# Weight sums for a seven-product matrix multiply: subtracting on VectorE, or adding while they are loaded

## The chip, the cores and the metric

One core of a Trainium2 chip runs one decoder layer as one program. The metric is the device time of one execution in microseconds (us), as the median of repeated runs. Engines: PE (TensorE matmuls), DVE (VectorE), ACT (ScalarE), POOL (GpSimd), SP (SyncE); the last two only issue transfers in the part of the kernel that matters here.

## The reference, cut to what matters

The layer normalises its input, makes one wide projection, runs two token mixers side by side (gated DeltaNet, block attention), and joins them. The change touches the joining part, for 256 tokens, a model width of 2048 and mixer outputs `oa`, `ob` of width 1024:

```python
u_a = oa @ w_branch_a                   # (256,1024) @ (1024,2048)
u_b = ob @ w_branch_b
merged = sigmoid(gate_a) * u_a + sigmoid(gate_b) * u_b
y = merged @ w_out                      # (256,2048) @ (2048,2048)
out = x + rms_norm(y, post_norm_w)
```

All of it is float32. Every float32 operand of a matmul is split into a high part that the matmul takes exactly and a low rest, and three products (high·high, high·low, low·high) are summed.

## The kernel before

**Weights.** Each weight block of 512 rows by 512 columns (1024 KB) is loaded by SP into one of three `raw` buffers (`load`, line 794, or `proj_n`, line 347), cast by ACT to a high part (`split`, line 226), and the low part is formed by DVE (line 227). The matmuls (line 148) take both. SP can load the next block into a `raw` buffer only when the last reader of the old block is done. The order of PE is pinned to that of the program; small jobs of the other engines are put between the matmuls by queues of generators that advance by a tick after each group of matmuls.

**Seven products instead of eight.** `oa @ w_branch_a` is done for two pairs of 512 columns (stages `ua0` and `ua2`), and the upper half of `merged @ w_out` for one pair (stage `y`). In each stage a 256 by 1024 operand times a 1024 by 1024 weight is cut into quarters A11 to A22 and B11 to B22, and the four result quarters c11 to c22 (one PSUM bank each) come out of seven products of quarters (Winograd's form of Strassen's scheme), where eight would be the plain way. Three of the seven take sums or differences of the weights' quarters, and the last one, p4, takes a combination of all four. `seven` (line 799) writes out this order: p1 (`raw`), other work, p5 (`tq[0]`), p6 (`tq[1]`), other work, p2 (`raw`, B21), p7 (`tq[2]`), other work, p3 (`raw`, B22), other work, p4 (`tq[1]` again). The other work is four blocks of a gate projection in the `ua` stages (gate0 to gate3; 24 matmuls each) and a block of another output quarter in the `y` stage.

**Where the combinations come from.** Each stage has three 1024 KB tiles `tq[0..2]`. POOL loads B12, B22 and B11 into them, three plain transfers (`fetch`, line 753). DVE then forms the differences in place, six instructions on half tiles, some groups of matmuls later (`differences`, line 758, waits in `T_WAIT`, line 32). The fourth combination overwrites `tq[1]` between p6 and p4: two DVE instructions subtract it from the `raw` block of B21 (`difference`, line 815, executed at line 817), so this `raw` buffer is held until then. One slice of `tq[0]` also keeps a copy (`s5`) of a PSUM bank that DVE adds into others (lines 808 and 823).

**Places.** The tiles of `ua0` lie in the buffers `g1` (`tq_g`, holding `tq[0]` and `tq[2]`) and `z2` (`tq_z`, holding `tq[1]`), fetched in `solve` (line 1004). Those of `ua2` and `y` lie in `z0`, `z1`, `z2` (`tq`), fetched by `next_differences` (line 879) as soon as the last readers of these buffers are done: for `ua2` these are the attention's last products (`z1`), its last transposes (`z0`) and p4 of `ua0` (`z2`). POOL works its transfers off in order; one that waits holds up those behind it. After the last stage's tiles POOL also loads `hx` (the residual's input) and `postw`.

Of the kernel before, what the change touches and what calls it, by code (L numbers as in the profile page):

```python
# [8 lines left out]
F32 = mybir.dt.float32  # L9
# [3 lines left out]
ALU = mybir.AluOpType  # L13
AX = mybir.AxisListType

P = 128
# [12 lines left out]
LC_WAIT = 3.5  # L29
INV = (0.6, 2)  # L30
SLOW = 8
T_WAIT = (5, 7, 7)
V_WAIT = 8
SV_WAIT = 1
OS_WAIT = 3
# [40 lines left out]
def hybrid_layer(  # L76
# [15 lines left out]
    nc = tc.nc  # L92
# [13 lines left out]
    wo = w_out.rearrange("o d f -> (o d) f")  # L106
# [639 lines left out]
    oaT = [None]  # L746

    oas, tqs = [], []
    formed = []
    sq = Queue()  # L750
    extra.append(sq)

    def fetch(tq, w, c, i):

        rs, cs = (0, 512, 0)[i], (c + (1, 1, 0)[i]) * 512
        nc.gpsimd.dma_start(tq[i], w[rs : rs + 512, cs : cs + 512].rearrange("(k p) c -> p k c", p=P))

    def differences(tq, c, wait):
        yield wait
        for o, a, b in ((0, 0, 2), (1, 1, 0), (2, 1, 2)):  # L760
            for u in range(2):
                us = slice(2 * u, 2 * u + 2)
                pin(nc.vector.tensor_tensor(tq[o][:, us], tq[a][:, us], tq[b][:, us], op=ALU.subtract))
                yield 1
        formed.append(c)

# [27 lines left out]
        nc.sync.dma_start(raw, w[h * 512 : (h + 1) * 512, c * 512 : (c + 1) * 512].rearrange("(k p) c -> p k c", p=P))  # L796
        return raw

    def seven(quarter, s_, tq, w, c, banks, name, fill=lambda i: None, done=lambda b: None):
        c11, c12, c21, c22 = banks  # L800
        s5 = tq[0][:, 0]
        product([quarter(0, 0)], load(w, 0, c, name), [c21], [True], f"{name}p1")
        fill(0)
        product([s_[0]], tq[0], [c12], [True], f"{name}p5")
        nc.scalar.copy(c11, c21)
        product([s_[1]], tq[1], [c21], [False], f"{name}p6")

        dq.add(steps(lambda: nc.scalar.copy(s5, c12), lambda: nc.vector.tensor_tensor(c12, c21, s5, op=ALU.add)))
        fill(1)
        dq.drain()  # L810
        raw21 = load(w, 1, c, name)
        product([quarter(0, 1)], raw21, [c11], [False], f"{name}p2")
        product([s_[2]], tq[2], [c21], [False], f"{name}p7")

        def difference(u):
            us = slice(2 * u, 2 * u + 2)
            pin(nc.vector.tensor_tensor(tq[1][:, us], raw21[:, us], tq[1][:, us], op=ALU.subtract))

        dq.add(
            steps(  # L820
                lambda: difference(0),
                lambda: difference(1),
                lambda: nc.vector.tensor_tensor(c22, c21, s5, op=ALU.add),
                lambda: done(c11),
            )
        )
        fill(2)
        product([s_[3]], load(w, 1, c + 1, name), [c12], [False], f"{name}p3")
        dq.drain()
        dq.add(steps(lambda: done(c12), lambda: done(c22)))  # L830
        fill(3)
        product([quarter(1, 1)], tq[1], [c21], [False], f"{name}p4")
        dq.add(later(lambda: done(c21)))
# [5 lines left out]
    def steps(*fs):  # L839
        for f in fs:  # L840
            yield 0.5
            f()
# [4 lines left out]

    def branch_pair(i):
        c = 2 * i
        while not oas or c not in formed:  # L850
            sq.tick()
            gq.tick()
        if not fourth:
            for q in aq + bq:
                q.drain()
            early.close()
            fourth.append(ctx.enter_context(tc.tile_pool(name="wx", bufs=1)))
        c11, c12, c21, c22 = (acc_tile(f"a_ua{c}_{n}") for n in ("11", "12", "21", "22"))
        place = {id(c11): (c, 0), id(c12): (c + 1, 0), id(c21): (c, 1), id(c22): (c + 1, 1)}

        def done(b):
            cc, t = place[id(b)]
            nc.vector.tensor_tensor(ga(cc, t), ga(cc, t), b, op=ALU.mult)


        quarter = quarters(hT)
        n, g, col = (("ga", 3, CGA), ("gb", 2, CGB))[i]
        pts = [aux_tile(f"a_{n}{g}_{t}") for t in range(NT)]

        def gate(h):  # L870
            raw = load(w_in[:, col : col + D], h, g, n)
            product([quarter(0, h), quarter(1, h)], raw, pts, [h == 0] * 2, f"{n}{g}_{h}")
            if h == 3:
                for t in range(NT):
                    nc.scalar.activation(gate_place(n, g, t), pts[t], AF.Sigmoid, scale=rstd[:, t : t + 1])

        seven(quarters(oaT[0]), oas, tqs[-1], wa, c, (c11, c12, c21, c22), f"ua{c}", fill=gate, done=done)

    def next_differences(w, c):


        for q in aq + bq:
            q.drain()
        tqs.append([big.tile([P, 4, 512], F32, tag=f"z{i}", name=f"tq{len(tqs)}_{i}") for i in range(3)])
        for i in (2, 0, 1) if len(tqs) == 2 else (1, 0, 2):
            fetch(tqs[-1], w, c, i)
        formed.clear()
        sq.add(differences(tqs[-1], c, T_WAIT[len(tqs) - 1]))

    def solve():  # L890
        oT = big.tile([P, H, 2 * S], F32R, tag="u1", name="oaT")
# [63 lines left out]
        def turned_outputs(ozs):  # L955


            a = {}
            for t in (1, 0):
                for g in range(2):  # L960
                    pt = aux_tile(f"ot_{t}_{g}")
                    for hh in range(4):
                        tr(pt[:, hh * P : (hh + 1) * P], ozs[t][:, g, hh, :], ident)
                    a[t, g] = pt.rearrange("p (h n) -> p h n", n=P)
                for g in range(2):
                    ks = slice(4 * g, 4 * g + 4)
                    halved(oT[:, ks, t * P : (t + 1) * P], oT[:, ks, S + t * P : S + (t + 1) * P], a[t, g])
                yield 1
            oa_f = big.tile([P, 2, 4, P], F32, tag="tv", name="oa_f")
            x, y = (oa_f[:, i] for i in range(2))  # L970
            nc.scalar.copy(x, a[1, 1])
            nc.vector.tensor_tensor(a[1, 1], a[1, 0], x, op=ALU.add)
            nc.scalar.copy(y, a[0, 0])
            nc.vector.tensor_tensor(a[0, 0], a[1, 1], y, op=ALU.subtract)
            nc.scalar.copy(x, a[0, 0])
            yield 1
            nc.vector.tensor_tensor(a[0, 1], a[0, 1], x, op=ALU.subtract)
            nc.vector.tensor_tensor(a[1, 0], y, a[1, 0], op=ALU.subtract)
            yield 1
            sums = [None] * 4  # L980
            for i, o, tag in ((0, (1, 1), "tt"), (1, (0, 0), "tw"), (3, (0, 1), None), (2, (1, 0), "tv")):
                if tag:
                    tl = big.tile([P, 2, 4, P], F32R, tag=tag, name=f"oas_{i}")
                    sums[i] = tl[:, 0], tl[:, 1]
                else:
                    sums[i] = [wk.tile([P, 4, P], F32R, tag="s", name=f"oas_{i}_{n}") for n in ("hi", "lo")]
                halved(*sums[i], a[o])
                yield 1
            oas.extend(sums)
# [10 lines left out]
        obs.append(big.tile([P, H, 2 * S], F32R, tag="g0", name="obT"))  # L1000
        tg = big.tile([P, 2, 4, 512], F32, tag="g1", name="tq_g")
        tz = big.tile([P, 4, 512], F32, tag="z2", name="tq_z")
        tqs.append((tg[:, 0], tz, tg[:, 1]))
        for i in (0, 2, 1):
            fetch(tqs[0], wa, 0, i)
        sq.add(differences(tqs[0], 0, T_WAIT[0]))
        yield OS_WAIT
        while attended[0] < H:
            yield 0.5
# [95 lines left out]
    for blk in ORDER:  # L1105
        n, c = blk[:2].rstrip("0123456789"), int(blk[-1])
        if n in ("q", "kq"):
            if n == "kq":
                keys(c)
            queries(c)  # L1110
        elif n in ("zg", "zm"):
            silu_gate(n, c)
        elif n == "v":
            values(c)
        elif n == "mv":
            attention_values(c)
        elif n == "mk":
            attention(c)
        elif n == "ua":
            branch_pair(c)  # L1120
        else:
            sigmoid_gate(n, {"ga": CGA, "gb": CGB}[n], c)
        if n == "ua":
            next_differences(*((wa, 2), (wo, 0))[c])


    gq.drain()
# [10 lines left out]
    def merge(c):  # L1138
# [14 lines left out]
                nc.scalar.copy(sf[:, t], p3)  # L1153
            yield 0.5
        if c == 1:
            nc.vector.tensor_tensor(sf[:, 2], p3s[1], sf[:, 1], op=ALU.add)
            nc.vector.tensor_tensor(sf[:, 3], sf[:, 2], sf[:, 0], op=ALU.subtract)
            yield 0.5
            nc.vector.tensor_tensor(sf[:, 1], sf[:, 0], sf[:, 1], op=ALU.subtract)
            nc.vector.tensor_tensor(sf[:, 0], p3s[0], sf[:, 3], op=ALU.subtract)  # L1160
            for i, j in enumerate((2, 3, 1, 0)):
                yield 1
                nc.scalar.copy(SH[i], sf[:, j])
# [20 lines left out]
        if i < 3:  # L1184
            third(1 + i)

    while not formed or not summed:
        mq.tick()
        sq.tick()
    c11, c12, c21, c22 = (acc_tile(f"a_y{n}") for n in ("11", "12", "21", "22"))  # L1190
    seven(quarter, list(zip(SH, SL)), tqs[-1], wo, 0, (c11, c12, c21, c22), "y", fill=beside)

    postw = big.tile([P, D], F32, tag="z2", name="postw")
    nc.gpsimd.dma_start(postw, post_norm_w.broadcast_to([P, D]))
# [104 lines left out]
```

## Time and profile before

| what | value |
|---|---|
| time, median of 3 runs | 771.48 us (771.03 to 771.73) |
| the profiled execution's own time | 772.1 us |
| span inside it that the profile covers | 770.4 us |
| mean granted TensorE clock | 0.996 |
| PE busy | 761.0 us (99%) |
| DVE busy | 565.7 us (73%) |
| ACT busy | 435.3 us (57%) |
| read from HBM | 148.04 MB |

The profiled execution is 0.6 us slower than the median. In the page's rows, `a<-b,c` is an instruction that writes tile `a` and reads `b` and `c`; times are counted from the span's start. "DMA share" is the mean busy share of the core's 16 DMA engines in a stretch; it can come out a little over 1. Ends of matmuls are modelled, so the distance between starts tells more than their length.

### The profile page before, as it was taken

To read this page: it belongs to the slowest core of one execution; us is meant where nothing else is said; L and a number is where in the kernel's file an instruction comes from. 1 tells how busy PE (TensorE), PEld (TensorE's weight loads), DVE (VectorE), ACT (ScalarE), POOL (GpSimd) and SP (SyncE) were. 2 spreads that over 40 slices of the span, in tenths; PEclk is the share of its full clock that TensorE was granted. 3 is DMA by queue.
4 is the path that set the end of the run, shared out by engine and by line. 5 is a ranking of instruction groups with operands and counts; after the bars stand their busy time and mean duration, and the time that the engine had idled before them with its cause. 6 is when DMAs were issued, how large, how long until landed. Compare 5 with 4: busy or idle time off the path is not lost.

```text
span 770.4 us, 10406 instructions
## 1 busy us (share of the span) xinstructions
PE 761.0 (99%) x3941; PEld 650.0 (84%) x3941; DVE 565.7 (73%) x918; ACT 435.3 (57%) x660; POOL 35.0 (5%) x63
## 2 busy tenths in 40 slices
PE   9999999999999999999999999999999999999995
PEld 8998988899888888888898888788888888888884
DVE  6878669885978898775557876686658676888753
ACT  6776665657655664554456574554455544555731
POOL 4000001112000000002001000000000000000000
PEclk9999999999999999999999999999999999999998
DMA  8585675467655556668437356667544955385912
GB/s 291 188 262 193 198 205 172 136 178 211 200 183 196 186 180 203 185 197 204 127 110 270 129 202 220 217 218 251 187 163 179 367 186 197 116 300 184 334 49 110
DMA packets 94808, 151.87 MB, mean 197 GB/s; under 512 B 3365, under 2 KB 49062, under 8 KB 94246
## 3 DMA queue, kind: packets, MB, share of 16 engines
q1 hardware_dynamic: 90022, 134.41, 54.0%
q0 software_dynamic: 4128, 15.74, 6.1%
q10 hardware_dynamic: 608, 1.06, 0.4%
q8 instruction: 31, 0.51, 0.3%
q14 instruction: 19, 0.16, 0.1%
HBM read 148.04 MB, written 3.15 MB: 196 GB/s over the span
## 4 chain that ended last, share of the span: by engine, by line
PE 94%; ACT 2%; DVE 2%; DMA 1%; issue 0%; POOL 0%; DVEq 0%; POOLq 0%
PE a_gb L148 11%; PE a_ga L148 11%; PE a_y L148 11%; PE a_mq L148 6%; PE a_mk L148 6%; PE a_k L148 6%; PE a_ub L148 6%; PE a_zm L148 6%; PE a_zg L148 5%; PE a_mv L148 5%; PE a_ua L148 5%; PE a_q L148 4%; PE a_v L148 4%; PE s L148 1%; PE ms L148 1%; PE po L148 1%
## 5 line engine op out<-in xcount | busy, mean ns | idle before, releaser
L148 PE MATMUL a_ga<-hi_ga,hT 128*128 128x512 f32 x256 | 82.1, 394 | 0.0
L148 PE MATMUL a_gb<-hi_gb,hT 128*128 128x512 f32 x256 | 80.2, 390 | 0.0
L227 DVE TENSOR_TENSOR lo_gb<-raw_gb,hi_gb 128x1024 fp32r<-128x1024 f32 x32 | 38.9, 1224 | 25.0 <-ACT hi_gb L226 24.9
L148 PEld LDWEIGHTS a_gb<-hi_gb,hT 128*128 128x128 f32 x256 | 48.0, 188 | 10.6
L148 PEld LDWEIGHTS a_ga<-hi_ga,hT 128*128 128x128 f32 x256 | 48.1, 188 | 10.1
L226 ACT CAST hi_gb<-raw_gb 128x1024 fp32r<-128x1024 f32 x32 | 33.3, 1051 | 35.6 <-PE a_gb L148 26.5
L226 ACT CAST hi_ga<-raw_ga 128x1024 fp32r<-128x1024 f32 x32 | 33.7, 1055 | 32.6 <-PE a_ga L148 13.7
L227 DVE TENSOR_TENSOR lo_ga<-raw_ga,hi_ga 128x1024 fp32r<-128x1024 f32 x32 | 38.9, 1222 | 17.9 <-ACT hi_ga L226 17.5
L148 PE MATMUL a_ga<-lo_ga,hT 128*128 128x512 f32 x128 | 50.1, 392 | 0.1
L148 PE MATMUL a_gb<-lo_gb,hT 128*128 128x512 f32 x128 | 50.1, 391 | 0.0
L148 PE MATMUL a_zg<-hi_zg,hT 128*128 128x348 f32 (+1 forms) x192 | 47.1, 322 | 0.0
L148 PE MATMUL a_mq<-hT,hi_mq 128*128 128x512 f32 x128 | 47.0, 408 | 0.0
L148 PE MATMUL a_mk<-hT,hi_mk 128*128 128x512 f32 x128 | 46.2, 402 | 0.0
L148 PE MATMUL a_y<-hi_y,mT 128*128 128x512 f32 x144 | 46.1, 392 | 0.0
L148 PE MATMUL a_q<-hT,hi_q 128*128 128x512 f32 x128 | 45.9, 398 | 0.0
L148 PE MATMUL a_v<-hT,hi_v 128*128 128x512 f32 x128 | 45.3, 398 | 0.0
L148 PE MATMUL a_ub<-hi_ub,obT 128*128 128x512 f32 x128 | 41.3, 395 | 0.0
L148 PE MATMUL a_k<-hT,hi_k 128*128 128x512 f32 x128 | 40.7, 400 | 0.0
L148 PE MATMUL a_zm<-hi_zm,hT 128*128 128x512 f32 x128 | 40.5, 392 | 0.0
L148 PE MATMUL a_mv<-hi_mv,hT 128*128 128x512 f32 x128 | 40.1, 391 | 0.0
L148 PE MATMUL a_v<-hT,lo_v 128*128 128x256 f32 x128 | 36.1, 282 | 0.1
L148 PE MATMUL a_q<-hT,lo_q 128*128 128x256 f32 x128 | 35.9, 280 | 0.0
(384 smaller groups left out, 1975.6 us busy)
## 6 DMA issues: line engine op xcount, KB each, us to landing
raw_ga<-in_w_in_dram SPq DMA_DIRECT2D x16, 1024.0 KB, 5.1
raw_gb<-in_w_in_dram SPq DMA_DIRECT2D x16, 1024.0 KB, 6.0
raw_y<-in_w_out_dram SPq DMA_DIRECT2D x15, 1024.0 KB, 5.3
raw_q<-in_w_in_dram SPq DMA_DIRECT2D x8, 1024.0 KB, 5.6
raw_mv<-in_w_in_dram SPq DMA_DIRECT2D x8, 1024.0 KB, 5.1
raw_v<-in_w_in_dram SPq DMA_DIRECT2D x8, 1024.0 KB, 5.6
raw_zm<-in_w_in_dram SPq DMA_DIRECT2D x8, 1024.0 KB, 5.0
raw_mq<-in_w_in_dram SPq DMA_DIRECT2D x8, 1024.0 KB, 5.8
```

The lines of the kernel that those rows point to most:

```text
L148: return pin(nc.tensor.matmul(*args, **kwargs))
L226: nc.scalar.copy(hi, raw)
L227: nc.vector.tensor_tensor(lo, raw, hi.bitcast(F32), op=ALU.subtract)
```

## The change

The signs of the scheme are turned: all combinations of the weights' quarters become sums (B11+B12 in `tq[0]`, B11+B12+B22 in `tq[1]`, B12+B22 in `tq[2]`, and for p4 `tq[1]` plus B21), and the subtractions move to the activations' combinations and the result banks, where additions and subtractions are exchanged one for one. The sums are then formed by POOL's transfers: the first quarter is loaded plainly, and each further one by a transfer that adds to its tile (`accum_op`). Per stage that is 3 plain and 4 adding transfers in `fetch`, and one more adding transfer (B21 onto `tq[1]`) issued after p6. The 24 DVE instructions of lines 763 and 817 go, and with them the queue `sq`, `formed` and `T_WAIT`.

```diff
-    def fetch(tq, w, c, i):
-        rs, cs = (0, 512, 0)[i], (c + (1, 1, 0)[i]) * 512
-        nc.gpsimd.dma_start(tq[i], w[rs : rs + 512, cs : cs + 512].rearrange("(k p) c -> p k c", p=P))
-    def differences(tq, c, wait):
-        yield wait
-        for o, a, b in ((0, 0, 2), (1, 1, 0), (2, 1, 2)):
-            for u in range(2):
-                us = slice(2 * u, 2 * u + 2)
-                pin(nc.vector.tensor_tensor(tq[o][:, us], tq[a][:, us], tq[b][:, us], op=ALU.subtract))
-                yield 1
-        formed.append(c)
+    def fetch(tq, w, c, order=(0, 2, 1)):
+        b11, b12, b21, b22 = (
+            w[r * 512 : (r + 1) * 512, (c + x) * 512 : (c + x + 1) * 512].rearrange("(k p) c -> p k c", p=P)
+            for r in range(2)
+            for x in range(2)
+        )
+        parts = [b11, b12], [b11, b12, b22], [b12, b22]
+        for n in range(3):
+            for i in order:
+                if n < len(parts[i]):
+                    nc.gpsimd.dma_start(tq[i], parts[i][n], **({"accum_op": ALU.add} if n else {}))
+        return b21
...
-    def seven(quarter, s_, tq, w, c, banks, name, fill=lambda i: None, done=lambda b: None):
+    def seven(quarter, s_, tq, b21, w, c, banks, name, fill=lambda i: None, done=lambda b: None):
...
-        dq.add(steps(lambda: nc.scalar.copy(s5, c12), lambda: nc.vector.tensor_tensor(c12, c21, s5, op=ALU.add)))
+        dq.add(steps(lambda: nc.scalar.copy(s5, c12), lambda: nc.vector.tensor_tensor(c12, s5, c21, op=ALU.subtract)))
+        nc.gpsimd.dma_start(tq[1], b21, accum_op=ALU.add)
         fill(1)
         dq.drain()
-        raw21 = load(w, 1, c, name)
-        product([quarter(0, 1)], raw21, [c11], [False], f"{name}p2")
+        product([quarter(0, 1)], load(w, 1, c, name), [c11], [False], f"{name}p2")
         product([s_[2]], tq[2], [c21], [False], f"{name}p7")
-        def difference(u):
-            us = slice(2 * u, 2 * u + 2)
-            pin(nc.vector.tensor_tensor(tq[1][:, us], raw21[:, us], tq[1][:, us], op=ALU.subtract))
-        dq.add(
-            steps(
-                lambda: difference(0),
-                lambda: difference(1),
-                lambda: nc.vector.tensor_tensor(c22, c21, s5, op=ALU.add),
-                lambda: done(c11),
-            )
-        )
+        dq.add(steps(lambda: nc.vector.tensor_tensor(c22, s5, c21, op=ALU.subtract), lambda: done(c11)))
...
-    def next_differences(w, c):
+    def next_sums(w, c):
...
-        for i in (2, 0, 1) if len(tqs) == 2 else (1, 0, 2):
-            fetch(tqs[-1], w, c, i)
-        formed.clear()
-        sq.add(differences(tqs[-1], c, T_WAIT[len(tqs) - 1]))
+        tqs.append((tq, fetch(tq, w, c)))
```

More of the change, by code (lines that the diff above doesn't have):

```diff
@@ L31 @@
 SLOW = 8
-T_WAIT = (5, 7, 7)
 V_WAIT = 8
@@ L748, in hybrid_layer @@
     oas, tqs = [], []
-    formed = []
-    sq = Queue()
-    extra.append(sq)
-    def fetch(tq, w, c, i):
-        rs, cs = (0, 512, 0)[i], (c + (1, 1, 0)[i]) * 512
-        nc.gpsimd.dma_start(tq[i], w[rs : rs + 512, cs : cs + 512].rearrange("(k p) c -> p k c", p=P))
-    def differences(tq, c, wait):
-        yield wait
-        for o, a, b in ((0, 0, 2), (1, 1, 0), (2, 1, 2)):
-            for u in range(2):
-                us = slice(2 * u, 2 * u + 2)
-                pin(nc.vector.tensor_tensor(tq[o][:, us], tq[a][:, us], tq[b][:, us], op=ALU.subtract))
-                yield 1
-        formed.append(c)
+    def fetch(tq, w, c, order=(0, 2, 1)):
[10 more added lines that the diff above has]
+        return b21
     def product(a, raw, banks, first, name):
@@ L849, in branch_pair @@
         c = 2 * i
-        while not oas or c not in formed:
-            sq.tick()
+        while not oas:
             gq.tick()
@@ L875, in gate @@
                     nc.scalar.activation(gate_place(n, g, t), pts[t], AF.Sigmoid, scale=rstd[:, t : t + 1])
-        seven(quarters(oaT[0]), oas, tqs[-1], wa, c, (c11, c12, c21, c22), f"ua{c}", fill=gate, done=done)
-    def next_differences(w, c):
+        seven(quarters(oaT[0]), oas, *tqs[-1], wa, c, (c11, c12, c21, c22), f"ua{c}", fill=gate, done=done)
+    def next_sums(w, c):
         for q in aq + bq:
             q.drain()
-        tqs.append([big.tile([P, 4, 512], F32, tag=f"z{i}", name=f"tq{len(tqs)}_{i}") for i in range(3)])
-        for i in (2, 0, 1) if len(tqs) == 2 else (1, 0, 2):
-            fetch(tqs[-1], w, c, i)
-        formed.clear()
-        sq.add(differences(tqs[-1], c, T_WAIT[len(tqs) - 1]))
+        tq = [big.tile([P, 4, 512], F32, tag=f"z{i}", name=f"tq{len(tqs)}_{i}") for i in range(3)]
+        tqs.append((tq, fetch(tq, w, c)))
     def solve():
@@ L971, in turned_outputs @@
             nc.scalar.copy(x, a[1, 1])
-            nc.vector.tensor_tensor(a[1, 1], a[1, 0], x, op=ALU.add)
+            nc.vector.tensor_tensor(a[1, 1], a[1, 0], x, op=ALU.subtract)
             nc.scalar.copy(y, a[0, 0])
@@ L976, in turned_outputs @@
             yield 1
-            nc.vector.tensor_tensor(a[0, 1], a[0, 1], x, op=ALU.subtract)
+            nc.vector.tensor_tensor(a[0, 1], a[0, 1], x, op=ALU.add)
             nc.vector.tensor_tensor(a[1, 0], y, a[1, 0], op=ALU.subtract)
@@ L1002, in solve @@
         tz = big.tile([P, 4, 512], F32, tag="z2", name="tq_z")
[L1003 to L1006, printed above, removed]
+        tq = tg[:, 0], tz, tg[:, 1]
+        tqs.append((tq, fetch(tq, wa, 0)))
         yield OS_WAIT
@@ L1123, in hybrid_layer @@
         if n == "ua":
-            next_differences(*((wa, 2), (wo, 0))[c])
+            next_sums(*((wa, 2), (wo, 0))[c])
     gq.drain()
@@ L1155, in merge @@
         if c == 1:
-            nc.vector.tensor_tensor(sf[:, 2], p3s[1], sf[:, 1], op=ALU.add)
+            nc.vector.tensor_tensor(sf[:, 2], sf[:, 1], p3s[1], op=ALU.subtract)
             nc.vector.tensor_tensor(sf[:, 3], sf[:, 2], sf[:, 0], op=ALU.subtract)
@@ L1159, in merge @@
             nc.vector.tensor_tensor(sf[:, 1], sf[:, 0], sf[:, 1], op=ALU.subtract)
-            nc.vector.tensor_tensor(sf[:, 0], p3s[0], sf[:, 3], op=ALU.subtract)
+            nc.vector.tensor_tensor(sf[:, 0], p3s[0], sf[:, 3], op=ALU.add)
             for i, j in enumerate((2, 3, 1, 0)):
@@ L1185, in beside @@
             third(1 + i)
-    while not formed or not summed:
+    while not summed:
         mq.tick()
-        sq.tick()
     c11, c12, c21, c22 = (acc_tile(f"a_y{n}") for n in ("11", "12", "21", "22"))
-    seven(quarter, list(zip(SH, SL)), tqs[-1], wo, 0, (c11, c12, c21, c22), "y", fill=beside)
+    seven(quarter, list(zip(SH, SL)), *tqs[-1], wo, 0, (c11, c12, c21, c22), "y", fill=beside)
     postw = big.tile([P, D], F32, tag="z2", name="postw")
```

## The prediction

> **What bounds the kernel now.** First the page's busy times and its chain, then the list of PE's waits, then a table of the three stages.
>
> ```profile
> span 770.4 us, 10406 instructions
> ...
> PE 761.0 (99%) x3941; PEld 650.0 (84%) x3941; DVE 565.7 (73%) x918; ACT 435.3 (57%) x660; POOL 35.0 (5%) x63
> ...
> PE 94%; ACT 2%; DVE 2%; DMA 1%; issue 0%; POOL 0%; DVEq 0%; POOLq 0%
> ```
> ```profile
> PE warm L148 <- DVE epst L182: 1.1, 1, 1.1
> ```
> ```profile
> 482.00:530.00 48.00, 47.91 (x209) 38.67 (x208) 35.05 (x34) 27.58 (x29) 0.75 (x1) 1.00 0.67 237
> 568.00:610.00 42.00, 42.00 (x185) 34.30 (x184) 32.02 (x31) 25.08 (x27) 2.25 (x3) 1.00 0.62 226
> 683.00:720.00 37.00, 37.00 (x167) 30.37 (x166) 30.34 (x30) 23.41 (x26) 1.26 (x2) 1.00 0.65 229
> ```
>
> The chain is PE for 94% of the span, and PE's only listed wait is 1.1 us at the start. The table's columns are PE, weight loads, DVE, ACT, POOL, clock, DMA share and GB/s: in the stages that the change touches (`ua0`, `ua2`, `y`) PE is busy all the time, DVE at most 82% (30.34 of 37), and the DMA engines about two thirds. So work taken from DVE is worth only what PE loses to it, and a delay of what PE reads counts in full.
>
> **The change part by part.**
>
> *DVE's 24 instructions go.*
>
> ```profile
> L763 DVE TENSOR_TENSOR tq<-tq,tq x12: 1218/1218/1220, 533.3 to 632.7; 128x1024 f32<-128x1024 f32 x12
> ```
> ```profile
> L817 DVE TENSOR_TENSOR tq_z<-raw_ua,tq_z x2: 1217/1218/1218, 504.2 to 505.4; 128x1024 f32<-128x1024 f32 x2
> ```
> ```profile
> 514.22 0.39 PE L148 MATMUL a_ga<-hi_ga,hT 128*128 128x512 f32 x1
> 514.44 0.47 PE L148 MATMUL a_ga<-lo_ga,hT 128*128 128x512 f32 x1
> 514.76 0.62 PE L148 MATMUL a_ga<-hi_ga,hT 128*128 128x512 f32 x2
> ```
>
> 18 at line 763 and 6 at line 817, 1.218 us each, are 29.2 us of DVE. All lie beside a full PE. What PE lost shows in the distances between its starts: 0.22 us is usual, 0.32 us at 514.44, where gate3's block came late because its `raw` buffer was B21's, held for line 817. The same slip can be lost once per stage: 3 x 0.1, and I take 0.2 us as the gain. The exchanged additions and subtractions cost the same instruction. In the order lists of both builds PE, ACT and SP have the same instructions in the same order; DVE lacks the 24, with two multiplications by the gate moved by one place; only POOL's list grows.
>
> *POOL's transfers* go from 9 of 1024 KB to 24: 9 plain, 15 adding. An adding one waits until the transfer before it on the same tile has landed; POOL works in order, so its wait holds the next ones. No run so far has an adding transfer. The nearest rows:
>
> ```profile
> tq<-in_w_branch_a_dram POOLq DMA_DIRECT2D x3, 1024.0 KB, 5.6
> ...
> hx<-in_x_dram POOLq DMA_DIRECT2D x1, 2048.0 KB, 8.4
> ```
> ```profile
> DMA to landing us min/median/max: 5.4/7.7/9.8
> ```
> ```profile
> 412.00:414.00 2.00, 2.00 (x15) 1.82 (x14) 2.00 (x8) 1.97 (x3) 0.00 (x0) 1.00 1.03 411
> 486.00:488.00 2.00, 2.00 (x10) 1.63 (x9) 0.27 (x2) 1.10 (x2) 0.00 (x0) 1.00 1.02 413
> 488.00:490.00 2.00, 2.00 (x11) 1.59 (x10) 1.20 (x1) 0.73 (x2) 0.00 (x0) 1.00 1.02 379
> 492.00:496.00 4.00, 4.00 (x19) 3.26 (x18) 3.22 (x4) 3.42 (x5) 0.00 (x0) 1.00 0.02 4
> 500.00:506.00 6.00, 6.00 (x28) 4.92 (x27) 4.37 (x5) 4.22 (x4) 0.00 (x0) 1.00 0.00 0
> 508.00:512.00 4.00, 4.00 (x19) 3.24 (x18) 3.80 (x5) 0.00 (x0) 0.00 (x0) 1.00 0.97 355
> ```
>
> At DMA share 1 the engines move about 400 GB/s, so a plain block takes 2.6 us of them. Call W the engine time of an adding block. Lower bound: the add is free, W = 2.6. Upper bound: the slowest landing of a line 756 transfer, 9.8. An add must fetch the weights and the tile, 2048 KB; `hx` is the only row of that size, and 1024 KB more take 8.4 - 5.4 = 3.0 us. I take W = 6.0, at the wide side of twice a block.
>
> The Trainium skill, "Collectives: The Full Stack", section "The bandwidth ceiling: the fold count and why AG ≠ RS ≠ AR", says that a DMA add is slow because of its two reads and not because of the sum (measured ratio 1.93); times 2.6 that is an estimate of 5.0, by which the sum below would end with a stall of 0 to 0.7 us.
>
> *The point where it decides: B21's add in `ua0`.* It must land between p6's last read and p4's first cast.
>
> ```profile
> 476.67 0.75 POOL L756 DMA_DIRECT2D tq<-in_w_branch_a_dram  x1 [61.71 <-PE po L148]
> 481.24 0.75 POOL L756 DMA_DIRECT2D tq<-in_w_branch_a_dram  x1 [3.82 <-PE pt L151]
> 518.66 0.75 POOL L756 DMA_DIRECT2D tq<-in_w_branch_a_dram  x1 [36.67 <-DVE lo_ua0p L227]
> 588.54 0.75 POOL L756 DMA_DIRECT2D tq<-in_w_out_dram  x1 [69.13 <-DVE lo_ua2p L227]
> ```
> ```profile
> 490.78 1.23 DVE L227 TENSOR_TENSOR lo_ua0p<-tq_z,hi_ua0p 128x1024 fp32r<-128x1024 f32 x1 [1.57 <-ACT hi_ua0p L226]
> ```
> ```profile
> L226 ACT CAST hi_ua0p<-tq_z x4: 1040/1048/1050, 486.9 to 514.9; 128x1024 fp32r<-128x1024 f32 x4
> ```
> ```profile
> 519.85 0.39 PE L148 MATMUL a_ua<-hi_ua0p,oaT 128*128 128x512 f32 x1
> 520.07 0.40 PE L148 MATMUL a_ua<-lo_ua0p,oaT 128*128 128x512 f32 x1
> ```
> ```profile
> 495.26 0.37 SPq L796 DMA_DIRECT2D raw_ua<-in_w_branch_a_dram  x1
> 506.66 0.37 SPq L796 DMA_DIRECT2D raw_ga<-in_w_in_dram  x1
> 507.76 0.37 SPq L352 DMA_DIRECT2D raw_gb<-in_w_in_dram  x1
> ```
>
> p6 has read its tile at 492.0. But in POOL's list of the changed build this add stands behind five transfers for `ua2`: B11 into `tq[1]` (476.67), B11 into `tq[0]` (481.24), then the first add to `tq[1]`, the add to `tq[0]`, the second add to `tq[1]`. This last one waits for the landing of the first. PE needs p4's low part at 520.07; less a cast (1.05), a subtraction (1.23) and two handovers of 0.04, the add may land at 517.7.
>
> At 488.0 the two plain fetches are through (413 GB/s before it). Gate2's load (2.6, the 379 GB/s row) and the first add (6.0) end at 496.6; the second add and B21's follow into the queue. Then come three adds (18.0), p3's load of 495.26 (2.6) and gate3's, which now leaves when p2's block is split, near 498, and not at 506.66 (2.6): 519.8. The load of 507.76 shares the engines with them: up to 2.6 more, 522.4. The idle stretches of before (492 to 496, 500 to 506) are filled. **Stall: 2.1 to 4.7 us, taken 3.4.** Behind the waiting cast on ACT stand the casts of the next gate's block, which PE needs 2.7 us later; they take 1.05 us each, so nothing is added.
>
> *The other adds have time.* In `ua2` and `y` B21's add has nothing unfinished ahead of it, and by the distances of `ua0` 25.7 us (492.0 to 517.7) for a landing like that of `hx`, 8.4. `ua0`'s own fetch starts 408 and is first cast after 482; `y`'s starts at 588.54 and is first cast after 683. `hx` and `postw` keep their releasers. I cost these at nothing; cover gone, each is worth its lateness.
>
> *The sum*, from the profiled execution: 772.1 - 0.2 + 3.4 = 775.3 us; it lay 0.6 above the median of the runs (772.1 against 771.48), so **774.7 us**.
>
> **The rivals.**
>
> *The adds fit (not slower).* By the same terms the add lands between 495.8 + 4W and, with the third load in full, 498.4 + 4W; that is 517.7 for W = 5.5 and 4.8. Below this no stall is left, and the time is 772.1 - 0.2 - 0.6 = 771.3. For it: the edge lies right beside twice a plain block (5.2), and PE's list has no wait on a transfer. Against: 3.0 us per block in the `hx` row. The ratio of the Trainium skill's page above belongs to this rival.
>
> *Raw loads starve.* Adds and SP's loads share the engines.
>
> ```profile
> q0 software_dynamic: 246, 0.99, 65.0%
> q1 hardware_dynamic: 284, 0.55, 37.6%
> ```
> ```profile
> 594.00:624.00 30.00, 30.00 (x133) 24.52 (x132) 22.08 (x22) 14.51 (x15) 1.45 (x2) 1.00 0.89 326
> ```
>
> In 598 to 602, with both queues full, POOL's (q0) had 65% of the time. The four adds of `y`'s fetch fall into a stretch with share 0.89 and are 24 us of engine time. At 37% a load takes 2.6 / 0.37 = 7.0 us, and gate blocks are used one per 24 matmuls, 24 x 0.23 = 5.5 us: 1.5 us lost per load, for some five loads (24 / 0.65 / 7.0), 7.5 us, less the lead of two further `raw` buffers, 2 x 5.5 less a landing of 5.6: 2.1 us, 773.4 if it comes alone. The Trainium skill, "DMA: Bandwidth & Descriptors", section "Queues, rings and completion order", says that an engine takes its queues in turn, packet by packet; a queue with larger packets then gets the larger share, with which the two rows agree (0.99 MB in 246 packets against 0.55 MB in 284).
>
> *The adds are far slower*, W = 9.8 or more: 495.8 + 39.2 = 535.0 or 537.6, 17 to 20 us late: 790 or more.
>
> *The change doesn't do what it says*: excluded for DVE by the order list; for faster by more than 0.2% PE would have to have 1.5 us to lose to DVE, and its starts show 0.3.
>
> **How the numbers follow.** A difference of 0.2% (1.5 us) is about what can be told from no change here. Chances: forecast 0.45, adds fit 0.37, loads starve alone 0.07, far slower 0.08, faster 0.03. Slower: 0.45 + 0.07 + 0.08 = 0.60; same 0.37; faster 0.03. The forecast's own range is 773 to 779 (a stall of 1.7 to 7.7 us, W from 5.4 to 7.0). The range has to take in the no-stall case, so it goes from 770.9 to 783 (a stall of 11.7 us, W near 8); it leaves out the far slower case and little else.
>
> **What would show it.** Right: in the changed profile PE waits near 520 for `lo_ua0p`, ACT before it for a transfer into `tq_z`, which lands after 518; DMA share near 1 from 484 to 520; adds landing 8 us or more after issue; 29 us less DVE. Wrong: that add landing before 517 (W below 5), or PE waiting first on a `raw` block, or a stall in `ua2` or `y`.

## The result, and the profile after

| | before | after |
|---|---|---|
| time, median of 4 runs each (before measured again) | 771.35 us (771.03 to 771.73) | 777.36 us (776.91 to 778.09) |
| ratio | | 1.0079, 95% interval 1.0061 to 1.0096 |
| the profiled execution | 772.1 us, span 770.4 | 776.95 us, span 775.2 |
| DVE busy | 565.7 us | 539.1 us |
| read from HBM | 148.04 MB | 163.77 MB |

The kernel became 6.0 us slower by the medians and 4.85 us slower between the two profiled executions (that of before lay 0.75 us above its median, that of after 0.4 below). The forecast was 774.7 us, inside a range of 770.9 to 783. All rows below are of the changed kernel until another is named. In it the matmul is line 147, the cast line 225, the low part line 226 and B21's add line 807.

The page, for the busy times, the queue of POOL's transfers (packets, MB, share of the 16 engines' span) and the chain:

```profile
span 775.2 us, 10408 instructions
...
PE 762.6 (98%) x3941; PEld 650.8 (84%) x3941; DVE 539.1 (70%) x894; ACT 434.6 (56%) x660; POOL 54.6 (7%) x78
...
q0 software_dynamic: 12048, 31.47, 17.3%
...
PE 93%; DMA 2%; ACT 2%; DVE 1%; issue 0%; DVEq 0%; ACTq 0%
```

DVE has lost its 24 instructions, and PE has nearly the busy time of before (762.6 against 761.0 us) in a longer span. In the chain DMA has 2% where it had 1%. The list of PE's waits tells where a transfer is late:

```profile
PE a_ga L147 <- ACT hi_ga L225: 2.6, 1, 2.6
PE warm L147 <- DVE epst L181: 1.1, 1, 1.1
PE a_ga L147 <- DVE lo_ga L226: 0.8, 1, 0.8
```

The wait of 1.1 us at the start was there before. Neither of the other two is at p4, where the forecast had put the stall. Both are at a gate block, once each. The chain for 476 to 530 (start, us, what) names the block:

```profile
497.58 17.69 DMA raw_ga<-in_w_in_dram
...
515.38 1.05 ACT hi_ga L225
...
516.45 1.24 DVE lo_ga L226
...
517.73 7.17 PE a_ga L147 x23
```

This is the raw load of gate3 in `ua0`. SP issued it at 497.58, 9 us earlier than before (506.66), and yet it landed only at 515.3. In the kernel before, the slowest load into this tile took 7.6 us. The last line of the tile's view, first of before, then of after:

```profile
DMA to landing us min/median/max: 5.0/5.1/7.6
```
```profile
DMA to landing us min/median/max: 5.0/7.1/17.7
```

PE had nothing else to do, since its order is fixed. Its last matmul ahead of the wait, in the timeline:

```profile
513.45 0.39 PE L147 MATMUL a_ua<-hi_ua0p,oas_lo 128*128 128x512 f32 x1
```

After the wait it was slow for a while. In the table of stretches, first of after, then of before, the clock (third column from the right) was 0.57 in 518 to 522, where the kernel before had 1.00, and PE started 12 matmuls there instead of 19:

```profile
518.00:522.00 4.00, 4.00 (x12) 3.10 (x12) 0.81 (x1) 0.85 (x1) 0.00 (x0) 0.57 1.05 356
```
```profile
518.00:522.00 4.00, 4.00 (x19) 3.26 (x18) 1.85 (x3) 2.94 (x5) 0.75 (x1) 1.00 0.87 308
```

The account of the profiled pair: at its usual distance of 0.23 us PE would have started the second matmul after 513.45 at 513.91; it started at 517.73, 3.8 us late. Seven matmuls fewer in the four slow microseconds, at 0.23 us each, are 1.6 us. The stage had begun 0.55 us earlier than before (SP's load of `raw_ua` at 494.71 against 495.26). 3.8 + 1.6 - 0.55 = 4.85 us, which is the difference measured.

And B21's add, the transfer on which the forecast rested? POOL's timeline and ACT's (start, duration, and in brackets the idle time before it and what ended it):

```profile
481.93 1.31 POOL L761 DMA_DIRECT2D tq<-in_w_branch_a_dram  x1 [0.42 <-DMA tq<-in_w_branch_a_dram]
489.15 1.29 POOL L761 DMA_DIRECT2D tq<-in_w_branch_a_dram  x1 [5.90 <-DMA tq<-in_w_branch_a_dram]
498.54 1.29 POOL L761 DMA_DIRECT2D tq<-in_w_branch_a_dram  x1 [8.10 <-DMA tq<-in_w_branch_a_dram]
499.28 1.85 POOL L807 DMA_DIRECT2D tq_z<-in_w_branch_a_dram  x1
```
```profile
515.38 1.99 ACT L225 CAST hi_ga<-raw_ga 128x1024 fp32r<-128x1024 f32 x2 [5.99 <-DMA raw_ga<-in_w_in_dram]
521.15 2.00 ACT L225 CAST hi_ua0p<-tq_z 128x1024 fp32r<-128x1024 f32 x2 [3.78 <-DMA tq_z<-in_w_branch_a_dram]
```

It stood behind three adds for `ua2` and landed at 521.1, inside the forecast's 519.8 to 522.4. The limit was 517.7 less the 0.55 by which the stage began earlier, so it was 3.9 us late. PE did not see it, because gate3's block had just delayed PE by more than that (3.8 and 1.6 us). So the profile of the changed kernel holds two late transfers, and the wait list shows only the first.

Why a load took 17.7 us shows in the DMA view (packets, MB, share of the engines' time), in a stretch in which both queues had work throughout (505 to 515), and in one in which an add was alone (586 to 588, a table row):

```profile
q0 software_dynamic: 657, 1.31, 70.6%
q1 hardware_dynamic: 655, 1.30, 39.1%
```
```profile
586.00:588.00 2.00, 2.00 (x10) 1.66 (x9) 2.00 (x3) 0.38 (x1) 0.00 (x0) 1.00 1.13 207
```

Alone, an adding transfer writes 207 GB/s. Beside SP's loads the two queues get equal numbers of packets of about 2000 bytes, hence 131 GB/s each, but a packet of the adds holds an engine 1.8 times as long (70.6 against 39.1). SP's loads fall from some 400 GB/s, which the engines moved in the kernel before when their share was 1, to 131: to a third.

Behind the rows: by the Trainium skill, "DMA: Bandwidth & Descriptors", section "Queues, rings and completion order", an engine goes round its queues packet by packet. The trace agrees, 657 packets to 655.

### The profile page after: what moved, and what is told of

Same layout as the page of the kernel before. It is cut to its first block, busy times and chain, and to the rows that moved or that the text cites. A ratio compares the mean times of both kernels' runs of the same rounds, so it can differ in the third digit from the quotient of the medians.

```text
span 775.2 us, 10408 instructions
## 1 busy us (share of the span) xinstructions
PE 762.6 (98%) x3941; PEld 650.8 (84%) x3941; DVE 539.1 (70%) x894; ACT 434.6 (56%) x660; POOL 54.6 (7%) x78
## 3 DMA queue, kind: packets, MB, share of 16 engines
q0 software_dynamic: 12048, 31.47, 17.3%
HBM read 163.77 MB, written 3.15 MB: 215 GB/s over the span
## 4 chain that ended last, share of the span: by engine, by line
PE 93%; DMA 2%; ACT 2%; DVE 1%; issue 0%; DVEq 0%; ACTq 0%
PE a_gb L147 11%; PE a_y L147 11%; PE a_ga L147 10%; PE a_zg L147 6%; PE a_mq L147 6%; PE a_k L147 6%; PE a_v L147 6%; PE a_mk L147 6%; PE a_ub L147 6%; PE a_zm L147 6%; PE a_mv L147 5%; PE a_q L147 4%; PE a_ua L147 3%; DMA raw_ga<-in_w_in_dram 2%; PE s L147 1%; PE ms L147 1%
## 5 line engine op out<-in xcount | busy, mean ns | idle before, releaser
L226 DVE TENSOR_TENSOR lo_ga<-raw_ga,hi_ga 128x1024 fp32r<-128x1024 f32 x32 | 39.1, 1223 | 26.2 <-ACT hi_ga L225 25.7
```

Source lines behind the costliest of these rows:

```text
L226: nc.vector.tensor_tensor(lo, raw, hi.bitcast(F32), op=ALU.subtract)
```

## The experiments

Theory A is the forecast's: the loss is B21's add in `ua0`, late because POOL's order puts it behind the adds of `ua2`. Theory B: it is gate3's load, starved by adds beside it, whatever their order. The times of before, measured beside these runs, were 771.26, 771.49 and 771.40 us for the first four, the next four and the last three. Ratios are to those, with 95% intervals.

**x1: B21's add first.** Each adding transfer of `ua2` is tied behind B21's add on POOL.

```diff
-                    nc.gpsimd.dma_start(tq[i], parts[i][n], **({"accum_op": ALU.add} if n else {}))
+                    load_ = nc.gpsimd.dma_start(tq[i], parts[i][n], **({"accum_op": ALU.add} if n else {}))
+                    if len(tqs) == 1 and n:
+                        behind(load_, last[0])
...
-        nc.gpsimd.dma_start(tq[1], b21, accum_op=ALU.add)
+        last[0] = nc.gpsimd.dma_start(tq[1], b21, accum_op=ALU.add)
```

> Same transfers as the changed kernel, but on POOL the adding transfer of the last block of `ua0` (the one p4 reads) goes ahead of the three adding transfers of `ua2`. Theory A (the forecast's step 3: this transfer is late because it is queued behind the others): it then lands some 10 to 15 us sooner, p4 waits for nothing, 771.0 to 772.0 us. Theory B (SP's load of the fourth gate block, issued at 497.58 in the trace of the changed kernel and cast only from 515.38, is starved because adding transfers share the DMA engines with it): four adding transfers still lie between 488 and 518, only in another order, so PE's wait in front of the gate matmuls stays, 2 to 4 us long, and the time is 775 to 778 us.

Measured: 779.36 us, ratio 1.0102 (1.0087 to 1.0117). PE's waits and ACT's cast of gate3's block in this run:

```profile
PE a_ga L147 <- ACT hi_ga L225: 3.2, 1, 3.2
...
PE a_ga L147 <- DVE lo_ga L226: 0.7, 1, 0.7
```
```profile
517.15 1.99 ACT L225 CAST hi_ga<-raw_ga 128x1024 fp32r<-128x1024 f32 x2 [5.59 <-DMA raw_ga<-in_w_in_dram]
```

Removing what A calls the cause made it worse by 2 us. The add of B21 now landed at 500.8 (issued 492.18, 8.6 us to landing), in time, but gate3's block came 1.8 us later still and the half clock lasted longer (0.50 in 520 to 524). A alone falls. The time is 1.4 us over B's interval.

The tie does more than exchange two places, as POOL's timeline and a row of stretches of this run show:

```profile
492.18 1.31 POOL L815 DMA_DIRECT2D tq_z<-in_w_branch_a_dram  x1 [10.24 <-DVE lo_ua0p L226]
492.96 3.17 POOL L767 DMA_DIRECT2D tq<-in_w_branch_a_dram  x2
```
```profile
492.00:494.00 2.00, 2.00 (x11) 1.64 (x10) 1.34 (x2) 1.69 (x4) 1.82 (x3) 1.00 0.04 8
```

The first add for `ua2`, issued at 481.93 in the changed kernel, now waits with the others until p6 has read its tile. Meanwhile the DMA engines run nearly empty (share 0.04 in 492 to 494, where the changed kernel has 1.08), and then three adds follow each other directly: they take 83.6% of the engines' time in 494 to 511, against 71.4% in the changed kernel, while gate3's load is under way. So x1 is not a clean exchange; x2 tests A without this.

**x2: no add of B21 in `ua0`.**

```diff
-        nc.gpsimd.dma_start(tq[1], b21, accum_op=ALU.add)
+        if name != "ua0":
+            nc.gpsimd.dma_start(tq[1], b21, accum_op=ALU.add)
```

> The changed kernel without the adding transfer of the last block in `ua0` (p4 of `ua0` is then computed without that block). Theory A: what was late is not there at all, 771.0 to 771.6 us. Theory B: the three adding transfers of `ua2` still share the engines with SP's load of the fourth gate block; in the trace of the changed kernel the two sides moved about the same number of bytes while both had work (a total of 260 to 290 GB/s), and the last transfer left only at 499.28 behind two others, so it had little part in the first 12 us of that load: its wait shortens by at most 1 us, 774.5 to 777 us.

Measured: 774.06 us (773.03 to 777.00), ratio 1.0042 (1.0025 to 1.0060). The profiled execution, 777.0, was the slowest of five. In it gate3's block is late by 1.9 and 0.8 us:

```profile
PE a_ga L147 <- ACT hi_ga L225: 1.9, 1, 1.9
...
PE a_ga L147 <- DVE lo_ga L226: 0.8, 1, 0.8
PE a_gb L147 <- DVE lo_gb L226: 0.7, 1, 0.7
```
```profile
518.00:520.00 2.00, 2.00 (x6) 1.57 (x5) 2.00 (x3) 0.41 (x1) 0.00 (x0) 0.50 0.45 86
```

So about half of the loss stays in the median when B21's add is not there at all, and gate3's block is late without it: B's mechanism costs by itself. The third wait, of 0.7 us, lies elsewhere, near 629, beside the adds for `y` (see x3). The median is 0.4 us under B's interval. Only the slowest execution has a profile, so how the 2.8 us of the median divide between the two places is not shown.

**x3: the sums of `ua2` on DVE.** `ua2` uses plain transfers and six DVE instructions, as before the change; everything else is as changed.

```diff
+    def fetch_plain(tq, w, c):
+        for i in ((0, 2, 1), (1, 0, 2), (2, 0, 1))[len(tqs)]:
...
+            nc.gpsimd.dma_start(tq[i], w[rows, cols].rearrange("(k p) c -> p k c", p=P))
+        sq.add(sums_on_dve(tq, (5, 7, 7)[len(tqs)]))
...
-        tqs.append((tq, fetch(tq, w, c)))
+        tqs.append((tq, (fetch_plain if len(tqs) in (1,) else fetch)(tq, w, c)))
```

> The three sums of `ua2` are formed by VectorE from plain transfers, as in the kernel before; all other sums stay with the transfers. Theories A and B both take the adding transfers of `ua2` for the cause (A through the queue behind them, B through the bytes beside SP's load): the wait at the fourth gate block goes, p4's block lands in time, 771.0 to 771.8 us. If the loss came from the adding transfers elsewhere (`ua0`'s own, those of `y`), 774 us or more stays.

Measured: 772.48 us, ratio 1.0017 (1.0008 to 1.0027). The waits in `ua0` are gone, and with them 4.8 of the 6.0 us: they need the adds of `ua2`. 1.2 us remain that neither theory had. They lie in the other place with four adds beside loads, the fetch for `y`, where a block of gate b came late:

```profile
PE a_gb L147 <- DVE lo_gb L226: 0.8, 1, 0.8
```
```profile
622.48 2.00 ACT L225 CAST hi_gb<-raw_gb 128x1024 fp32r<-128x1024 f32 x2 [4.71 <-DMA raw_gb<-in_w_in_dram]
```

**x4: all transfers plain.** The same 24 transfers in the same places, none of which adds.

```diff
-                    nc.gpsimd.dma_start(tq[i], parts[i][n], **({"accum_op": ALU.add} if n else {}))
+                    nc.gpsimd.dma_start(tq[i], parts[i][n])
...
-        nc.gpsimd.dma_start(tq[1], b21, accum_op=ALU.add)
+        nc.gpsimd.dma_start(tq[1], b21)
```

> All 24 transfers into the tiles of weights stay, at the same places of the same queue, but none adds (each overwrites its tile, so no sum of weights is formed). Theory B with the addition as its price: a plain transfer moves its block in about half the engine time (4096 bytes per packet in the trace of before), the load of the fourth gate block lands by 510, 771.0 to 772.0 us. If the additional 15.7 MB of reads as such is the price, whether they add or not: 774 us or more.

Measured: 771.23 us, ratio 0.9998 (0.9989 to 1.0008). POOL's queue in its page, and the cast of gate3's block:

```profile
q0 software_dynamic: 8208, 31.47, 11.6%
```
```profile
508.73 1.05 ACT L225 CAST hi_ga<-raw_ga 128x1024 fp32r<-128x1024 f32 x1 [0.67 <-DMA raw_ga<-in_w_in_dram]
```

The bytes are the same 31.47 MB, but the time of the engines is 11.6% instead of 17.3%. The price is not the 15.7 MB more that are read; it is that the transfers add. This run has a second use: DVE is rid of its 24 instructions here and nothing is late, so it shows what that relief is worth. It is nothing that can be measured (the interval allows at most 0.85 us).

**x5: one add ahead, the others after p4.** Of the three adds for `ua2` that stood ahead of B21's one stays there; the others are tied, each behind the transfer issued before it in the program, and so come after `tq[2]`'s first load, which waits for p4.

```diff
-                    nc.gpsimd.dma_start(tq[i], parts[i][n], **({"accum_op": ALU.add} if n else {}))
+                    load_ = nc.gpsimd.dma_start(tq[i], parts[i][n], **({"accum_op": ALU.add} if n else {}))
+                    if len(tqs) == 1 and (n or i == 2):
+                        pin(load_)
...
-        nc.gpsimd.dma_start(tq[1], b21, accum_op=ALU.add)
+        added = nc.gpsimd.dma_start(tq[1], b21, accum_op=ALU.add)
+        if name == "ua0":
+            pin(added)
```

> Same transfers as the changed kernel, in another order on POOL: of the three adding transfers of `ua2` one stays ahead of the last block of `ua0`, and the others wait until p4 of `ua0` has read its tile. Theory B (adding transfers beside SP's loads starve them): two adding transfers instead of four lie between 489 and 516, the load of the fourth gate block gets the engines to itself from about 506 and lands by 510, the wait goes there; 771.5 to 773.5 us, if the three that now run after 516 don't starve the `raw_gb` loads in their turn (774 or more if they do). Theory A (order on POOL alone): 771.0 to 772.0 us.

Measured: 771.40 us, ratio 1.0000 (0.9991 to 1.0010): the change as a whole, all 15 adds, without its loss. PE's list has only the waits of the start; gate3's block and B21's are cast in time:

```profile
509.16 1.05 ACT L225 CAST hi_ga<-raw_ga 128x1024 fp32r<-128x1024 f32 x1 [0.69 <-DMA raw_ga<-in_w_in_dram]
...
512.53 1.06 ACT L225 CAST hi_ua0p<-tq_z 128x1024 fp32r<-128x1024 f32 x1 [0.33 <-PE a_ua L147]
```

The time is in A's interval and 0.1 us under B's; what tells these two apart is x1 and x2, not this run. The four adds of `y` are in this run too, and the load beside them was cast at 620.75, by which PE lost nothing. In x3 it was 622.48. So `y`'s fetch stands at the edge.

**x6 and x6b: is the half clock a consequence of idling?** 40, then 14 idle matmuls are put on PE ahead of gate3's.

```diff
+        if name == "ua0":
+            warm2 = aux_tile("warm2")
+            for i in range(14):
+                mm(warm2[:, :P], ones, ones, start=True, stop=True)
         fill(3)
```

> The changed kernel with 40 matmuls of 128 columns into a spare bank put on TensorE ahead of the fourth gate block's matmuls, where it waits (they do about 2.2 us of idle work, and the kernel's result is the same). In the trace of the changed kernel, first matmuls start 427 ns apart instead of 227 for 3.4 us after the wait, at a granted clock of 0.5. If that half clock comes from TensorE having been idle, it goes, and with it 1.5 to 1.7 us: 775.0 to 776.0 us. If it comes from something else (the load itself, the phase of the run), the time stays at 777 to 778 us.

Measured: 780.49 us, ratio 1.0119 (1.0104 to 1.0134), outside both intervals: I had mis-sized the filler. Its row shows 80 instructions and 9.1 us, not 2.2:

```profile
513.91 9.09 PE L147 MATMUL warm<-ones 128*128 128x128 f32 x80
```

> The filler run again with 14 matmuls in place of 40, since one of them took two passes of 113 ns, not 55 ns in all: 3.1 us of idle work in the 2.8 us gap ahead of the fourth gate block. The 40 kept the granted clock at 1.0, and 8.9 us of filler took the place of 2.8 + 1.0 us of waiting and 1.65 us of half clock: 776.95 + 3.4 = 780.4 us by this account, measured 780.49. So the clock falls because TensorE idles, and 14 should give 1.65 us back, less up to 0.9 us because the last block of `ua0`, landing near 521, then comes late for p4: 775.3 to 776.6 us. If the half clock stays: 777 to 778 us.

Measured: 775.20 us, ratio 1.0049 (1.0032 to 1.0066), 2.2 us less than the changed kernel and 0.1 under the first interval. The clock's row, against 0.57 above:

```profile
518.00:522.00 4.00, 4.00 (x19) 3.24 (x18) 0.70 (x1) 0.47 (x1) 0.00 (x0) 1.00 1.07 354
```

This profile is of the slowest of the four executions (776.38 us; the others took 775.0 to 775.4). In its list PE waits for gate3's low part and, at p4, for B21's, whose lateness was covered in the changed kernel:

```profile
PE a_ga L147 <- DVE lo_ga L226: 0.5, 1, 0.5
PE a_ua L147 <- DVE lo_ua0p L226: 0.4, 1, 0.4
```

Work that computes nothing makes the kernel faster, because PE doesn't idle: the half clock is a consequence of the wait, and 1.6 us of the loss by the account above.

**x8: gate3's load on a third queue.** Only this load is issued on ACT's queue.

```diff
-    def load(w, h, c, name):
+    def load(w, h, c, name, queue=nc.sync):
...
-        nc.sync.dma_start(raw, w[h * 512 : (h + 1) * 512, c * 512 : (c + 1) * 512].rearrange("(k p) c -> p k c", p=P))
+        queue.dma_start(raw, w[h * 512 : (h + 1) * 512, c * 512 : (c + 1) * 512].rearrange("(k p) c -> p k c", p=P))
...
-            raw = load(w_in[:, col : col + D], h, g, n)
+            raw = load(w_in[:, col : col + D], h, g, n, nc.scalar if i == 0 and h == 3 else nc.sync)
```

> The changed kernel with only the load of the fourth gate block of `ua0` issued on ScalarE's queue instead of SP's; bytes, moments and all adding transfers stay. Theory B in its narrow form (the engines take a packet from each queue in turn, so that SP's two loads share one half and the adding transfers have the other): three queues have a third each while all have work, the load no longer stands behind the one of `raw_ua` and lands at 508 to 512, its wait is at most 1 us, 771.5 to 774.5 us. If only the sum of bytes counts, or the two queues of plain loads share one turn, it lands as late as before (514 or later): 776 to 778 us.

Measured: 779.39 us, ratio 1.0103 (1.0086 to 1.0120). The load came in time, as the narrow form of B says. But the time didn't follow:

```profile
511.92 2.00 ACT L225 CAST hi_ga<-raw_ga 128x1024 fp32r<-128x1024 f32 x2 [1.09 <-DMA raw_ga<-in_w_in_dram]
523.20 1.99 ACT L225 CAST hi_ua0p<-tq_z 128x1024 fp32r<-128x1024 f32 x2 [9.29 <-DMA tq_z<-in_w_branch_a_dram]
```
```profile
PE a_ua L147 <- ACT hi_ua0p L225: 4.4, 1, 4.4
...
PE a_ua L147 <- DVE lo_ua0p L226: 0.5, 1, 0.5
```

Here is theory A's stall, at p4, as forecast, and larger, since a third queue (q10) took packets beside the adds; the half clock follows it (0.50 in 524 to 528). In 504 to 511 of this run:

```profile
q0 software_dynamic: 389, 0.79, 61.0%
q10 hardware_dynamic: 354, 0.70, 27.5%
q1 hardware_dynamic: 254, 0.49, 21.2%
```

The turns are not exact thirds, but the adds, with half of the packets before, have 39% here (389 of 997). Each of the two late transfers hides the other; to take one away uncovers the other or feeds it. Call this theory C.

**x10: x1 and x8 together. x11: x2 and x8 together.**

> Both moves at once: the adding transfer of the last block of `ua0` ahead of those of `ua2` on POOL, which alone gave 779.4 us, and the load of the fourth gate block on ScalarE's queue, which alone gave 779.4 us. Two late arrivals, each of which hides the other (theory C: the fourth gate block's load, needed by about 512, and the last block of `ua0`, needed by about 517): with each move the one arrival comes in time and the other later, so together both come in time and only the load of `raw_ua`, a third of the engines wide, can still be a little late: 771.3 to 774.5 us. If the moves themselves cost (an order, a queue on ScalarE), their losses of 8 us add or stay: 779 us or more.

Measured: 775.73 us, ratio 1.0056 (1.0041 to 1.0071). Two losses of 8 us became one of 4.3 us, so they don't add; but it lies over C's interval. The chain names a third transfer, p3's `raw` load, for which PE waited 1.2 and 0.8 us. And the gap of x1 is here too, in the row of stretches:

```profile
494.61 16.38 DMA raw_ua<-in_w_branch_a_dram
```
```profile
490.00:492.00 2.00, 2.00 (x10) 1.69 (x9) 1.71 (x2) 1.36 (x3) 0.34 (x1) 1.00 0.00 0
```

The DMA engines stood idle, and then three adds were issued from 491.66 on, ahead of p3's load at 494.61. Theory C had not asked what the move of x1 does to the adds that it puts off.

> The load of the fourth gate block on ScalarE's queue, and the adding transfer of the last block left out in `ua0` (p4 of `ua0` is computed without that block). Alone, the second gave 774.1 us (773.0 to 777.0) and the first 779.4 us, with a wait of 4.4 us for that block. Theory C: with the load in time and the block not there, nothing is late: 771.2 to 772.5 us. If a third cause in this stretch was hidden (the half clock without a wait, the later casts), 773.5 us or more.

Measured: 772.31 us, ratio 1.0015 (1.0006 to 1.0025). With one add left out, three queues and no gap, nothing is late by more than 0.2 us in PE's list, and 0.9 us remain (PE starts 17 matmuls in 508 to 512 and 17 in 512 to 516, where x9 has 19 in each). The bytes of the adds alone don't decide: in 488 to 520 x10 has 3.15 MB of them and x11 3.01. How full the stretch is with four, the changed kernel's queues show for 488 to 520:

```profile
q0 software_dynamic: 2073, 4.11, 69.2%
q1 hardware_dynamic: 2192, 4.36, 40.0%
```

The engines were busy all through these 32 us (the shares can sum to a little over 1), about 20 us of it for adds (69.2 of 109.2). x5 takes two of the four adds out of the stretch and pays nothing. Whether some order with all four ahead of p4 would lose nothing is not shown: x1 and x10 leave the engines idle first.

**x9: adds for B21 only.** All sums on DVE but the last block of each stage: the edit of x3 for all three stages.

> All sums of `ua0`, `ua2` and `y` by VectorE as in the kernel before, except the last block of each of the three products of seven, which an adding transfer brings (three adding transfers in place of twelve). The run with plain transfers in `ua2` alone kept 1.2 us over the kernel before and a wait of 0.8 us for a `raw_gb` block near 624, beside the adding transfers of `y`. If those are the rest, it goes here: 770.9 to 771.6 us. If the last blocks' adding transfers or VectorE's sums cost it, 772 us or more stays.

Measured: 771.26 us, ratio 0.9997 (0.9988 to 1.0007). Without four adds in a row nothing is lost, in `y` either. The rest of x3 is put down to the adds of `y` by the place of its wait; no run leaves out these alone, and x5 has them and loses nothing.

No version was measurably faster than the kernel before: x4 (which forms no sums), x5 and x9 equal it.

## Why the prediction was right, and where not

*DVE's 24 instructions.* They went, and DVE's busy time fell by 26.6 us, not by 29.2: the forecast added up durations, and neighbouring instructions of DVE overlap a little (in the kernel before one of 1.22 us starts at 532.13 and the next at 533.27). The 0.2 us of gain can't be told from nothing: x4 has 771.23 us against 771.26.

*W, the engine time of an add.* Taken as 6.0 us. Alone it is 1.05 MB / 207 GB/s = 5.1 us, 1.95 times a plain block's 2.6. The size was wide by 0.9. The Trainium skill's ratio in "Collectives: The Full Stack", section "The bandwidth ceiling: the fold count and why AG ≠ RS ≠ AR", 1.93 between two collectives, agrees with the trace's 1.95; the estimate of 5.0 from it was nearer than my value. The forecast's "W from 5.4 to 7.0" doesn't come out of its own sum: stalls of 1.7 and 7.7 us need 5.6 and 7.1.

*B21's add in `ua0`.* The queue order, the filled stretches and the landing (521.1 for 519.8 to 522.4) came out. Two errors of size cancelled in it. Between 488 and 520 the trace has 4.11 MB of adds and 4.36 MB of loads, 3.9 adds and 4.2 loads: 3.9 x 5.1 + 4.2 x 2.6 = 30.8 us of the 32. The forecast had 4 x 6.0 and three loads, 31.8, and a fourth load only as its upper end. The lateness itself is real, as x8 and x6b show, but in the changed kernel it is covered.

*The step that failed* is the one inside this sum: gate3's load, "which now leaves when p2's block is split, near 498, and not at 506.66 (2.6)". I entered it as 2.6 us that delay B21's add and did not ask when it would land itself. It was needed by about 511.6 to 512.5 (PE's first and second matmul were due at 513.68 and 513.91; less a cast of 1.05, for the second also a low part of 1.23, and handovers), and at a third of the rate it landed at 515.3. To leave 9 us earlier did not help: beside the adds the load took 17.7 us where it had taken at most 7.6.

*The rivals.* That raw loads starve was the second rival, and this is what happened. That a load's share of the engines was put at 37% and came out at 36% (39.1 of 109.7) is in part luck: the 37% were read beside plain transfers, whose packets are twice as large (0.99 MB in 246), while the packets of adds are as large as the loads' and hold an engine longer. And the rival was put in the wrong place. I looked for it at `y`'s fetch, where it is at the edge (nothing in x5, 1.2 us in x3), and not in `ua0`, where I had just filled the same stretch with four adds. "PE waiting first on a `raw` block" was named as what would show the forecast wrong, and that is what PE's list shows. "The adds fit" is out: W lies inside its bounds (4.8 to 5.5), and there was still a loss.

*The half clock* was in no term. It is 1.6 us of the changed kernel's loss; x6b, which avoids it, is 2.2 us faster.

*The other adds.* "Have time" holds for `ua2`'s B21 and for `hx`; for `y` only just.

So the sign and the place within 10 us were right, and a stall of 3.4 us stood for one of 5.4 (3.8 and 1.6): a different transfer, with the clock's fall behind it. That the time lies in the range says little, since the range went from no change to 11 us more; that it lies near the forecast is in part luck, since the transfer for which the sum was made never stopped PE.

## What to carry to other kernels

When transfers are added beside loads, ask of every transfer in the stretch when it lands at its queue's share of the engines, not only of the one that the change is about; a sum of engine time has no deadlines in it. If the first late transfer is mended and the time doesn't follow, look for the second one that it hid, compare the work in the stretch with the stretch before moving orders and queues about, and see that a move doesn't first leave the engines idle (x1, x10). To relieve an engine that was not on the chain (DVE at 73%) was worth nothing that could be measured here, and a transfer that adds was paid for in the time of the DMA engines.

## What the runs showed of the hardware

- An adding transfer of 1024 KB took 5.1 us of the 16 engines (207 GB/s written), a plain one 2.6 (at some 400 GB/s). Over the whole kernel the same 31.47 MB took 12048 packets and 17.3% of the engines' time with 15 adds, 8208 packets and 11.6% without.
- With adds and loads side by side the queues got 657 and 655 packets in 10 us, 131 GB/s each.
- The issue of an adding transfer held POOL 1.27 to 1.33 us, a plain one 0.75 to 0.79.
- PE's clock fell to a half after a short wait: 2.6 and 0.8 us in the changed kernel, 1.9 and 0.8 us in x2, 1.2 and 0.8 us in x10 (0.50 in 516 to 518). A single wait of 0.8 us, in x3, left it at 1.00. The Trainium skill, "TensorE: Matmul & The Clock Gate", section "What's actually happening", has the clock fall to a half after at least one idle window of about 3.4 us. The size of the fall agrees (0.50 in x2's row); the idle time that was enough here is shorter, two waits with one matmul between them.
